# A two-block transformer forward pass on one core: last outputs in tiles of their own, first units side by side, the end reordered

## The chip, the cores and the metric

The kernel runs on 1 core of one Trainium2 chip. The metric is the device time of one execution in microseconds (us). The core's engines are TensorE (PE in the profile, with PEld for its weight loads), VectorE (DVE), ScalarE (ACT), GpSimd (POOL) and SyncE (SP), which issues the transfers of weights.

## The reference

One sequence of 512 tokens by 1024 features, all in float32. `first_block` runs a mixer (sparse attention and gated linear attention, merged), attention over a memory of 256 tokens, a gated FFN with a convolution over tokens, and a norm. `second_block` then runs retention, an FFN, stick-breaking attention, an FFN, and the final norm:

```python
def _rmsnorm(x, g):
    xf = x.astype(jnp.float32)
    y = xf * lax.rsqrt(jnp.mean(xf * xf, axis=-1, keepdims=True) + EPS)
    return (y * g.astype(jnp.float32)).astype(x.dtype)
...
    for i in range(DEPTH_2):
        j = i // N_MIXERS
        if i % N_MIXERS == 0:
            x = x + _retention(_rmsnorm(x, ret_norm[j]), ret_w_in[j], ret_w_out[j])
        else:
            x = x + _stick_breaking(_rmsnorm(x, sb_norm[j]), sb_w_in[j], sb_w_out[j])
        x = x + _conv_ffn(_rmsnorm(x, ffn_norm[i]), ffn_w_up[i], ffn_conv_w[i],
                          ffn_conv_b[i], ffn_w_down[i])
    return _rmsnorm(x, final_norm)
```

Retention has 4 heads with 256 key and 512 value features, stick-breaking attention 16 heads of 64 (here 8 pairs), each FFN 2816 hidden features (two up-projections, a convolution of width 3, a product, a down-projection).

## The kernel before, in words

**Number format.** Every float32 factor is split into a high part and a low part of a reduced type (fp32r). A product of two factors is then three matmuls: high by high (L184), high or low by low or high (L185, L186). In the rows, `xh` and `xl` are the parts of an activation, `wh` and `wl` those of a weight. In this text "a product" is one such matmul of 128x128 by 128x512.

**Activations.** x is kept transposed in SBUF: 8 tiles `x[0]` to `x[7]`, each 128 features by 512 tokens. For a norm, each is scaled by the norm's gain and split: ScalarE makes the high part (L276), VectorE the low part (L277). The parts of `x[0]` to `x[3]` lie in one tile (`xh_87`, `xl_89`), those of `x[4]` to `x[7]` in another (`xh_88`, `xl_90`). The scale of the norm (one number per token) comes later: ScalarE squares each x (L242), GpSimd adds the squares (L246, the last add on VectorE), TensorE adds over features ("column sums", L251), `rsqrt_cols` takes the root (L218 to L222, on VectorE with the power on GpSimd), TensorE broadcasts it over partitions (L231), ScalarE copies it to SBUF (`rB`, L269), and the products are scaled after the fact.

**Weights.** All weights are streamed once as "units" of 128x1024 (`wload`): SyncE starts the transfer into one of 2 raw buffers, ScalarE makes the high part (L157), VectorE the low part (L158), into rings of 3. A unit with 8 tiles of activations is 24 products into one PSUM bank (`fm_unit`). `norm_x` issues the splits, the first unit, the column sums, two more units, then the broadcast.

**Outputs.** Each stage ends with a projection whose results VectorE adds into x (L307). `out_proj2` takes half-length units, each for two outputs; `out_proj4` goes round four outputs in four banks.

**Stages.** `xat` (memory attention), `ffa` (first FFN), `ret` (retention), `ffb` (second FFN), `stk` (stick), `ffc` (third FFN). In retention each head makes keys, queries and values, the attention, and a gate; its result is transposed by TensorE and split into `yh`, `yl`; head 3 puts them into the tiles of `x[0]` to `x[3]`'s split. In stick the pairs 6 and 7 put their outputs into the tiles of `x[0]` and `x[1]`'s split.

**The end.** `down_halves` does the last down-projection's outputs 4 to 7 in two halves of 256 tokens, so that the final norm of half 0 (`finish`) runs beside the products of half 1. Five of eight outputs of a half are made by VectorE (L909), three by GpSimd (`POOL_TILES`, L907).

**What sets the order.** The kernel is written against a framework with a scheduler: a tool places each engine's instructions in an order of its own that respects the dependences between tiles and PSUM banks, and inserts the waits. So an engine's order differs from the order in the code, and a tile that is reused makes a wait. PSUM has 8 banks; the stages share them out by name (`pp` for products, `pa` for norms).

## Time and profile before

| | us |
|---|---|
| median of 3 runs | 2318.01 |
| lowest, highest of the runs | 2315.68, 2319.25 |
| the profiled execution | 2320.69 |
| its span in the trace | 2318.8 |
| TensorE busy | 2278.5 (98%) |
| VectorE busy | 1400.9 (60%) |
| ScalarE busy | 1022.5 (44%) |
| GpSimd busy | 194.5 (8%) |

The span is the time between the first and the last instruction in the trace. The mean granted clock of TensorE over the execution is 0.992 of full speed. A time line has one row per instruction or run of like instructions: start, duration, engine, line, operation, out <- in, and in brackets the idle time of the engine before it with what ended it. A TensorE row's duration overlaps its successor's, so the spacing of products is read from their starts.

### The profile page before, as it was taken

Reading aid. Unit: us, or ns where it says so; the run is one execution under the profiler, and the core shown is the slowest. Engines: PE = TensorE matmul, PEld = TensorE weight load, DVE = VectorE, ACT = ScalarE, POOL = GpSimd, SP = SyncE. Lnnn points to the kernel's source line nnn. Section 1 sums busy time; section 2 is a strip of 40 time slices with the busy share of each in tenths; the row PEclk is TensorE's granted clock in tenths of the full one; section 3 lists DMA queues with packets and bytes.
Section 4 is the critical chain, followed back from the end, with each engine's and each line's share of the span. In section 5 each row is a group of like instructions: output and inputs, shape, how many; then the busy total and the mean of one; then the engine's idle time right before and its main releaser. Section 6 shows DMA issues by size and latency. Waiting matters only on the chain.

```text
span 2318.8 us, 27885 instructions
## 1 busy us (share of the span) xinstructions
PE 2278.5 (98%) x10808; PEld 1880.6 (81%) x10808; DVE 1400.9 (60%) x2197; ACT 1022.5 (44%) x1665; POOL 194.5 (8%) x230
## 2 busy tenths in 40 slices
PE   9999999999999999999999999999999999999997
PEld 7787778877888888888887788888888887888886
DVE  5447875456545456445454674746577886747465
ACT  4345763444323244433333442424477884424243
POOL 2001110101000003000000100000121101000002
PEclk9989999999999999999999999999999999999998
DMA  5312133312232223222222233232343322232232
GB/s 160 91 55 63 37 119 96 123 63 95 97 100 94 98 88 114 90 91 78 81 96 73 82 100 99 92 100 93 98 126 93 92 67 80 100 100 92 100 93 71
DMA packets 66054, 213.41 MB, mean 92 GB/s; under 512 B 7793, under 2 KB 10114, under 8 KB 65794
## 3 DMA queue, kind: packets, MB, share of 16 engines
q1 hardware_dynamic: 60802, 203.24, 26.9%
q0 software_dynamic: 5120, 8.39, 1.6%
q8 instruction: 85, 1.39, 0.3%
q14 instruction: 47, 0.39, 0.1%
HBM read 201.11 MB, written 2.10 MB: 88 GB/s over the span
## 4 chain that ended last, share of the span: by engine, by line
PE 90%; DVE 4%; ACT 2%; POOL 1%; issue 1%; DMA 1%; SPq 0%; DVEq 0%; POOLq 0%; ACTq 0%
PE pp L184 26%; PE pp L186 26%; PE pp L185 26%; DVE wl L158 1%; PE po L701 1%; ACT pr L673 1%; DVE xl L277 1%; PE po L1163 1%; POOL pr L682 1%; PE pt L697 1%; PE pp L1070 1%; PE pp L1072 1%; PE pp L1071 1%; DVE x L307 1%; PE pa L1002 1%
## 5 line engine op out<-in xcount | busy, mean ns | idle before, releaser
L157 ACT ACTIVATE wh<-wr 128x1024 fp32r<-128x1024 f32 (+2 forms) x368 | 384.4, 1044 | 776.5 <-PE pp L185 609.0
L184 PE MATMUL pp<-xh,wh 128*128 128x512 f32 x1612 | 635.2, 394 | 3.4 <-ACT xh L276 3.2
L185 PE MATMUL pp<-xl,wh 128*128 128x512 f32 x1612 | 632.9, 393 | 3.6 <-DVE xl L277 3.6
L186 PE MATMUL pp<-xh,wl 128*128 128x512 f32 x1612 | 632.8, 393 | 0.0
L158 DVE TENSOR_TENSOR wl<-wr,wh 128x1024 fp32r<-128x1024 f32 (+2 forms) x368 | 451.6, 1227 | 211.5 <-ACT wh L157 185.2
L185 PEld LDWEIGHTS pp<-xl,wh 128*128 128x128 f32 x1612 | 305.0, 189 | 66.7 <-DVE xl L277 5.7
L184 PEld LDWEIGHTS pp<-xh,wh 128*128 128x128 f32 x1612 | 304.6, 189 | 66.7 <-ACT xh L276 4.4
L186 PEld LDWEIGHTS pp<-xh,wl 128*128 128x128 f32 x1612 | 304.6, 189 | 62.8 <-issue 0.9
L307 DVE TENSOR_TENSOR x<-x,pp 128x512 f32<-128x512 f32 x130 | 89.1, 686 | 230.2 <-PE pp L186 230.1
L184 PE MATMUL pp<-mid,wh 128*128 128x512 f32 x504 | 196.6, 390 | 0.3
L185 PE MATMUL pp<-mid,wh 128*128 128x512 f32 x504 | 196.1, 390 | 0.0
L186 PE MATMUL pp<-mid,wl 128*128 128x512 f32 x504 | 195.8, 389 | 0.0
L246 POOL TENSOR_TENSOR acc<-acc 128x512 f32<-128x512 f32 (+1 forms) x60 | 80.6, 1344 | 904.8 <-ACT acc L242 835.2
L185 PE MATMUL pp<-wl,xh 128*128 128x512 f32 (+1 forms) x320 | 123.0, 385 | 3.2 <-DVE wl L158 3.2
L184 PE MATMUL pp<-wh,xh 128*128 128x512 f32 (+1 forms) x320 | 121.8, 383 | 0.9 <-ACT wh L157 0.9
L186 PE MATMUL pp<-wh,xl 128*128 128x512 f32 (+1 forms) x320 | 122.1, 382 | 0.0
L184 PEld LDWEIGHTS pp<-mid,wh 128*128 128x128 f32 x504 | 94.6, 188 | 22.2 <-ACT mid L157 2.8
L185 PEld LDWEIGHTS pp<-mid,wh 128*128 128x128 f32 x504 | 94.6, 188 | 20.4 <-DVE mid L158 1.1
L186 PEld LDWEIGHTS pp<-mid,wl 128*128 128x128 f32 x504 | 94.6, 188 | 19.5
L157 ACT ACTIVATE mid<-wk 128x512 fp32r<-128x512 f32 x66 | 41.6, 631 | 124.4 <-DVE wk L874 108.7
L847 ACT ACTIVATE wk<-wk,vec 128x512 f32<-128x512 f32 x110 | 88.6, 809 | 6.6 <-DVE wk L861 5.2
L849 DVE SCALAR_TENSOR_TENSOR wk<-wk,vec 128x510 f32<-128x510 f32 x110 | 82.3, 750 | 3.6
(432 smaller groups left out, 3349.0 us busy)
## 6 DMA issues: line engine op xcount, KB each, us to landing
wr<-in_up SPq DMA_DIRECT2D x88, 512.0 KB, 3.3
wr<-in_w_up SPq DMA_DIRECT2D x44, 512.0 KB, 3.3
wr<-in_w_in_fm SPq DMA_DIRECT2D x32, 512.0 KB, 3.6
wr<-in_ret_vg SPq DMA_DIRECT2D x32, 512.0 KB, 3.3
wr<-in_down SPq DMA_DIRECT2D x32, 512.0 KB, 3.3
wr<-in_w_down SPq DMA_DIRECT2D x16, 512.0 KB, 3.3
wr<-in_ret_qk SPq DMA_DIRECT2D x16, 512.0 KB, 3.3
wr<-in_ret_out SPq DMA_DIRECT2D x16, 512.0 KB, 3.3
```

The costliest lines, as they stand in the source:

```text
L157: act.activation(hi, src, AF.Copy)
L158: dve.tensor_sub(lo, src, hi.bitcast(F32))
L184: pe.matmul(ps, sh, mh, start=first and i == 0, stop=False)
L185: pe.matmul(ps, sh, ml, start=False, stop=False)
L186: pe.matmul(ps, sl, mh, start=False, stop=last and i == n - 1)
L246: (dve if k == len(tiles) - 1 else pool).tensor_add(acc[:, :n], acc[:, :n], sq[:, :n])
L277: dve.scalar_tensor_tensor(lo, x, g, hi.bitcast(F32), op0=OP.mult, op1=OP.subtract)
L307: dve.tensor_add(xT[m], xT[m], ps)
L673: act.activation(dst, dst, AF.Exp, scale=-1.0, bias=nm[:, b:b + 1], accum_out=ss[:, g, b:b + 1])
L682: scaler(b).tensor_scalar(prs[g][b], prs[g][b], ss[:, g, b:b + 1], 1.0, op0=OP.mult, op1=OP.mult)
L847: act.activation(dst, src, AF.Identity, scale=V(wname, 2 * nw + j), bias=V(bname, j))
L849: dve.scalar_tensor_tensor(dst[:, 2:], src[:, :S - 2], V(wname, j), dst[:, 2:], op0=OP.mult, op1=OP.add)
```

## The change

It has four parts.

1. `norm_x` of the FFNs and of stick runs the first two units side by side (`two_units`): for each tile of activations, high part with both units' high and low parts, into two banks; then the 16 products with the low parts of the activations. The column sums come after both units. Memory attention keeps the old order.
2. Retention's values of a head lie in one tile for high and one for low parts; head 3's result goes into these and no longer into the tiles of `x[0]` to `x[3]`'s split. Stick's pairs 6 and 7 put their outputs into tiles of its values and queries.
3. Retention's head 0 makes the next head's keys ahead of its transposes; head 3 makes the first half of the previous head's output projection ahead of its own and the second half behind them.
4. The end: the norm scale of half 0 is computed during the products of half 1 but broadcast after the last of them; the last square is not added but summed by column sums of its own; VectorE's outputs take the broadcast from PSUM, six of eight outputs are VectorE's; 24 and 30 products of a 128x128 identity in bf16 (`warm`), whose results nobody reads, stand ahead of the column sums and of the broadcast of half 1.

```diff
-POOL_TILES = (2, 3, 5)
+POOL_TILES = (2, 5)
...
+    def two_units(srcs, h, tags):
+        us = [wload(u) for u in srcs]
+        pss = [bank(t) for t in tags[:2]]
+        for k in range(KD):
+            c = slice(k * P, (k + 1) * P)
+            for (hi, lo), ps in zip(us, pss):
+                pe.matmul(ps, hi[:, c], h[k][0], start=k == 0, stop=False)
+                pe.matmul(ps, lo[:, c], h[k][0], start=False, stop=False)
+        for k in range(KD):
+            c = slice(k * P, (k + 1) * P)
+            for (hi, lo), ps in zip(us, pss):
+                pe.matmul(ps, hi[:, c], h[k][1], start=False, stop=k == KD - 1)
+        return pss
+
-    def norm_x(gname, first, tags=("pp", "pp", "pp")):
+    def norm_x(gname, first, tags=("pp", "pp", "pp"), two=True):
...
-        ahead = []
+        ahead = two_units(first[:2], h, tags) if two else []
...
-        units(0, 1)
-        rcol, rB = norm_scale(xT, mid=lambda: units(1, 3))
+        units(len(ahead), 1)
+        rcol, rB = norm_scale(xT, mid=lambda: units(len(ahead), 3))
...
+        def warm(n):
+            ps = bank("pp")
+            for _ in range(n):
+                pe.matmul(ps[:, :P], identb, identb, start=True, stop=True)
...
+        def scales(ps, acc, last):
+            for x in range(n // P):
+                for i, t in enumerate((acc, last)):
+                    pe.matmul(ps[:, x:x + 1], t[:, x * P:(x + 1) * P], ones[:, 0:1], start=i == 0, stop=i == 1)
...
+        def outputs(half, rcol):
+            c = cols[half]
+            psb = bcast_cols(rcol[:, :n // P], n // P)
+            rB = sm.tile([P, S], F32, name="rB", bufs=1)
+            act.activation(rB[:, :n], psb[:, :n], AF.Copy)
...
-                        dve.scalar_tensor_tensor(y[:, j, :], xT[k][:, c], V("final_norm", k), rB[:, :n], op0=OP.mult,
+                        dve.scalar_tensor_tensor(y[:, j, :], xT[k][:, c], V("final_norm", k), psb[:, :n], op0=OP.mult,
                                                  op1=OP.mult)
...
-        finish(0, lambda: [product(1, i) for i in range(1, NHALF - 1)])
-        product(1, NHALF - 1)
-        finish(1)
+        r0 = scales(*sums(0))
+        for i in range(1, NHALF):
+            product(1, i)
+        s1 = sums(1)
+        outputs(0, r0)
+        warm(24)
+        r1 = scales(*s1)
+        warm(30)
+        outputs(1, r1)
...
+            vhl = [st.tile([P, NT, S], F32R, tag="v" + c, name="v" + c) for c in "hl"]
             for t in range(NT):
-                hi, lo = tiles(st, "v", 2, 8, F32R)
+                hi, lo = [x[:, t, :] for x in vhl]
...
-            if 0 < hd < 3:
-                out_proj2("ret_out", hd - 1, out_prev)
-            yh, yl = [st.tile([P, 4, S], F32R, tag="y" + c, name="y" + c) for c in "hl"] if hd < 3 else [x[0] for x in xhl]
+            if hd == 0:
+                ahead.append([fm_unit(wload(a["ret_qk"][10 + i]), h, KD) for i in range(2)])
+            else:
+                out_proj2("ret_out", hd - 1, out_prev, 0, 2 if hd == 3 else 4)
+            yh, yl = [st.tile([P, 4, S], F32R, tag=("y" if hd < 3 else "v") + c, name="y" + c) for c in "hl"]
...
-        out_proj2("ret_out", 2, ys[2])
+        out_proj2("ret_out", 2, ys[2], 2)
...
-            oh, ol = tiles(st, "os", 2, NOS, F32R) if pair < 6 else (xh[pair - 6], xl[pair - 6])
+            if pair < 6:
+                oh, ol = tiles(st, "os", 2, NOS, F32R)
+            elif pair == 6:
+                vt = st.tile([P, 3, 4, P], F32R, tag="vh", name="vh", bufs=2).rearrange("p t b d -> p t (b d)")
+                oh, ol = vt[:, 0, :], vt[:, 1, :]
+            else:
+                qt = st.tile([P, 2, S], F32R, tag="qh", name="qh", bufs=2)
+                oh, ol = qt[:, 0, :], qt[:, 1, :]
```

Three places show how the order moves. The first is VectorE from the last adds of retention's outputs into the second FFN (`x_3000` to `x_3014` in steps of 2 are x[0] to x[7]; `xl_89` and `xl_90` hold the low parts of x[0] to x[3] and x[4] to x[7]; `wl` is a weight unit's low part). Before:

```order
L307 TENSOR_TENSOR x_3006<-x_3006,pp 128x512
L158 TENSOR_TENSOR wl<-wr,wh 128x1024
L307 TENSOR_TENSOR x_3008<-x_3008,pp 128x512
L277 SCALAR_TENSOR_TENSOR xl_90<-x_3008,vec,xh_88 128x512
L307 TENSOR_TENSOR x_3010<-x_3010,pp 128x512
L158 TENSOR_TENSOR wl<-wr,wh 128x1024
L277 SCALAR_TENSOR_TENSOR xl_90<-x_3010,vec,xh_88 128x512
L307 TENSOR_TENSOR x_3012<-x_3012,pp 128x512
L277 SCALAR_TENSOR_TENSOR xl_89<-x_3000,vec,xh_87 128x512
L277 SCALAR_TENSOR_TENSOR xl_90<-x_3012,vec,xh_88 128x512
L277 SCALAR_TENSOR_TENSOR xl_89<-x_3002,vec,xh_87 128x512
L307 TENSOR_TENSOR x_3014<-x_3014,pp 128x512
```

With the change, the same place:

```order
L322 TENSOR_TENSOR x_3006<-x_3006,pp 128x512
L277 SCALAR_TENSOR_TENSOR xl_89<-x_3000,vec,xh_87 128x512
L277 SCALAR_TENSOR_TENSOR xl_89<-x_3002,vec,xh_87 128x512
L322 TENSOR_TENSOR x_3008<-x_3008,pp 128x512
L277 SCALAR_TENSOR_TENSOR xl_89<-x_3004,vec,xh_87 128x512
L277 SCALAR_TENSOR_TENSOR xl_89<-x_3006,vec,xh_87 128x512
L158 TENSOR_TENSOR wl<-wr,wh 128x1024
L322 TENSOR_TENSOR x_3010<-x_3010,pp 128x512
L277 SCALAR_TENSOR_TENSOR xl_90<-x_3008,vec,xh_88 128x512
L158 TENSOR_TENSOR wl<-wr,wh 128x1024
L322 TENSOR_TENSOR x_3012<-x_3012,pp 128x512
```

The low parts of x[0] to x[3] moved from behind the add of x[6] to ahead of the add of x[5].

The second is TensorE at the first FFN's first products (the numbers behind the names tell tiles and units apart; `xh0_87` and `xl0_89` are the tiles named above). Before, one unit:

```order
L184 MATMUL pp_4585<-xh0_87,wh_4580 128x512
L185 MATMUL pp_4585<-xl0_89,wh_4580 128x512
L186 MATMUL pp_4585<-xh0_87,wl_4581 128x512
L184 MATMUL pp_4585<-xh0_87,wh_4580 128x512
L185 MATMUL pp_4585<-xl0_89,wh_4580 128x512
```

With the change, the start of the block and the start of its second part:

```order
L286 MATMUL pp_4591<-xh0_87,wh_4580 128x512
L287 MATMUL pp_4591<-xh0_87,wl_4581 128x512
L286 MATMUL pp_4592<-xh0_87,wh_4586 128x512
L287 MATMUL pp_4592<-xh0_87,wl_4587 128x512
...
L291 MATMUL pp_4591<-xl0_89,wh_4580 128x512
L291 MATMUL pp_4592<-xl0_89,wh_4586 128x512
```

The products with low parts of the activations moved behind all products with high parts, and the second unit's weights (`wh_4586`, `wl_4587`) are read from the third product on.

The third is VectorE at the very end (`y` are outputs, `pa` the broadcast scale in PSUM, `rB` its copy). Before:

```order
L892 TENSOR_TENSOR x_3012<-x_3012,pp 128x256
L909 SCALAR_TENSOR_TENSOR y<-x_3000,vec,rB 128x256
L909 SCALAR_TENSOR_TENSOR y<-x_3002,vec,rB 128x256
L909 SCALAR_TENSOR_TENSOR y<-x_3008,vec,rB 128x256
L909 SCALAR_TENSOR_TENSOR y<-x_3012,vec,rB 128x256
L909 SCALAR_TENSOR_TENSOR y<-x_3014,vec,rB 128x256
L892 TENSOR_TENSOR x_3014<-x_3014,pp 128x256
L246 TENSOR_TENSOR acc<-acc 128x256
L218 TENSOR_SCALAR v<-pa 128x2
```

With the change:

```order
L246 TENSOR_TENSOR acc<-acc 128x256
L907 TENSOR_TENSOR x_3014<-x_3014,pp 128x256
L945 SCALAR_TENSOR_TENSOR y<-x_3000,vec,pa 128x256
L945 SCALAR_TENSOR_TENSOR y<-x_3002,vec,pa 128x256
L945 SCALAR_TENSOR_TENSOR y<-x_3006,vec,pa 128x256
L945 SCALAR_TENSOR_TENSOR y<-x_3008,vec,pa 128x256
L945 SCALAR_TENSOR_TENSOR y<-x_3012,vec,pa 128x256
L945 SCALAR_TENSOR_TENSOR y<-x_3014,vec,pa 128x256
L218 TENSOR_SCALAR v<-pa 128x2
```

The add of the last product moved ahead of half 0's outputs, and the last add of squares left its place between the last product's add and the norm scale.

## Rows read from the trace of the kernel before

**Rows 1.** Page: busy us (share of the span) and instructions of each engine

```profile
PE 2278.5 (98%) x10808; PEld 1880.6 (81%) x10808; DVE 1400.9 (60%) x2197; ACT 1022.5 (44%) x1665; POOL 194.5 (8%) x230
```

**Rows 2.** TensorE's waits: line waited for, releaser; us, times, longest us

```profile
PE pp L185 <- DVE xl L277: 3.6, 5, 1.2
PE pp L184 <- ACT xh L276: 3.2, 2, 2.8
PE pa L1036 <- DVE v L218: 1.7, 2, 0.9
PE pa L1036 <- DVE sg L1028: 1.3, 2, 0.6
```

**Rows 3.** Time line, TensorE, the end: start us, us, [idle before, releaser]

```profile
2305.84 0.99 PE L251 MATMUL pa<-cst,acc 128*128 128x1 f32 x4 [3.80 <-DVE acc L246]
2308.54 1.19 PE L231 MATMUL pa<-cst,rcol 128*128 128x128 f32 x4 [1.72 <-DVE rcol L222]
```

**Rows 4.** Stretches: us, busy by engine (instructions), granted clock, DMA share, GB/s

```profile
505.00:525.93 20.93, 20.93 (x89) 16.46 (x89) 14.10 (x16) 11.30 (x17) 6.40 (x4) 1.00 0.14 45
525.93:547.07 21.14, 19.71 (x83) 15.66 (x82) 10.42 (x14) 5.75 (x8) 5.12 (x4) 0.92 0.31 106
1296.71:1318.07 21.36, 18.83 (x83) 14.26 (x82) 11.29 (x17) 7.47 (x11) 2.37 (x2) 1.00 0.28 97
1662.71:1680.14 17.43, 17.43 (x83) 14.56 (x82) 6.20 (x10) 5.75 (x7) 1.05 (x2) 1.00 0.33 113
1932.63:1955.45 22.82, 19.82 (x83) 15.79 (x83) 9.55 (x15) 6.85 (x10) 2.32 (x2) 0.93 0.26 90
```

**Rows 5.** Time line, TensorE, first FFN

```profile
536.76 0.63 PE L186 MATMUL pp<-xh,wl 128*128 128x512 f32 x1
537.19 0.55 PE L184 MATMUL pp<-xh,wh 128*128 128x512 f32 x1
537.58 0.40 PE L185 MATMUL pp<-xl,wh 128*128 128x512 f32 x1
537.81 0.39 PE L186 MATMUL pp<-xh,wl 128*128 128x512 f32 x1
```

**Rows 6.** Time line, ScalarE, second FFN

```profile
1297.58 2.56 ACT L276 ACTIVATE xh<-x,vec 128x512 fp32r<-128x512 f32 x4 [1.98 <-DVE x L307]
```

**Rows 7.** Time line, TensorE, second FFN

```profile
1302.76 0.50 PE L185 MATMUL pp<-xl,wh 128*128 128x512 f32 x1 [0.72 <-DVE xl L277]
```

**Rows 8.** Time line, VectorE, ahead of the first FFN

```profile
525.14 2.32 DVE L158 TENSOR_TENSOR wl<-wr,wh 128x1024 fp32r<-128x1024 f32 x1
```

**Rows 9.** Time line, TensorE, third FFN

```profile
1935.58 0.73 PE L184 MATMUL pp<-xh,wh 128*128 128x512 f32 x2 [2.79 <-ACT xh L276]
```

**Rows 10.** Time line, VectorE, third FFN

```profile
1932.96 0.67 DVE L307 TENSOR_TENSOR x<-x,pp 128x512 f32<-128x512 f32 x1
```

**Rows 11.** Time line, VectorE, ahead of stick

```profile
1659.70 1.23 DVE L158 TENSOR_TENSOR wl<-wr,wh 128x1024 fp32r<-128x1024 f32 x1 [0.19 <-ACT wh L157]
```

**Rows 12.** Time line, TensorE, head 0 of retention

```profile
975.52 0.40 PE L184 MATMUL pp<-xh,wh 128*128 128x512 f32 x1
976.54 0.63 PE L1036 MATMUL pa<-cst,sg 128*128 128x128 f32 x4 [0.63 <-DVE sg L1028]
```

**Rows 13.** Time line, VectorE, the end

```profile
2300.36 3.96 DVE L909 SCALAR_TENSOR_TENSOR y<-x,vec,rB 128x256 f32<-128x256 f32 x5 [0.46 <-ACT rB L269]
2304.25 0.41 DVE L892 TENSOR_TENSOR x<-x,pp 128x256 f32<-128x256 f32 x1
2306.86 0.16 DVE L218 TENSOR_SCALAR v<-pa 128x2 f32<-128x2 f32 x1 [1.17 <-PE pa L251]
2310.27 3.56 DVE L909 SCALAR_TENSOR_TENSOR y<-x,vec,rB 128x256 f32<-128x256 f32 x5 [1.88 <-ACT rB L269]
```

**Rows 14.** Time line, TensorE, stick: a 128x128 bf16 product

```profile
1698.10 0.23 PE L1128 MATMUL zA<-maskb,identb 128*128 128x128 bf16 x1
1698.14 0.36 PE L1126 MATMUL zA<-qh,k 128*128 128x256 f32 x1
```

More of the change, by code (lines that the diff above doesn't have):

```diff
@@ L312, in out_proj, with out_proj2 @@
             add_x(m, ps)
-    def out_proj2(name, part, rhs, m0=0):
-        for m2 in range(m0, KD // 2):
+    def out_proj2(name, part, rhs, m0=0, m1=KD // 2):
+        for m2 in range(m0, m1):
             u = wload(a[name][part * 4 + m2])
@@ L793, in xattn @@
     def xattn(st, mkT, mv):
-        h, rcol, rB, ahead = norm_x("ln_x", [a["w_xq"][i] for i in range(3)])
+        h, rcol, rB, ahead = norm_x("ln_x", [a["w_xq"][i] for i in range(3)], two=False)
         os_ = []
@@ L892, in product, with sums @@
             dve.tensor_add(xT[m][:, c], xT[m][:, c], ps[:, :n])
[L894 to L901 removed]
+        def warm(n):
+            ps = bank("pp")
+            for _ in range(n):
+                pe.matmul(ps[:, :P], identb, identb, start=True, stop=True)
+        def sums(half):
+            c = cols[half]
+            ps = bank(cur["norm"])
+            acc = sumsq([x[:, c] for x in xT[:KD - 1]], n)
+            last = sm.tile([P, S], F32, tag="nrm", name="acc", bufs=3)
+            act.activation(last[:, :n], xT[KD - 1][:, c], AF.Square)
+            return ps, acc, last
+        def scales(ps, acc, last):
+            for x in range(n // P):
+                for i, t in enumerate((acc, last)):
+                    pe.matmul(ps[:, x:x + 1], t[:, x * P:(x + 1) * P], ones[:, 0:1], start=i == 0, stop=i == 1)
+            rcol = sm.tile([P, NT], F32, tag="rcol", name="rcol")
+            rsqrt_cols(rcol[:, :n // P], ps[:, :n // P], n // P, float(D), n // P)
+            return rcol
+        def outputs(half, rcol):
[3 more added lines that the diff above has]
+            act.activation(rB[:, :n], psb[:, :n], AF.Copy)
             for k2 in range(KD // 2):
```

13 lines of the change are left out of this document (4 added, 9 removed).

## The prediction

> **What bounds the kernel now.** I read the busy times first. TensorE is busy for 98% of the span [rows 1], so the other engines cost time only where TensorE waits for them or runs slowly because of them. The list of TensorE's waits, grouped by releaser, says where that is [rows 2]. It is short, and these kinds of wait in it belong to places that the change edits: low parts of the activations from the vector engine (3.6 us in five waits, one in the first FFN and four in the second), high parts from ScalarE (3.2 us in two, 2.8 of it in the third FFN), and the transposes of retention (1.7 and 1.3 us, half of each in head 0 and half in head 3). The time line of TensorE at the very end adds two more, 3.80 us before the last column sums and 1.72 before the last broadcast [rows 3].
>
> The waits do not tell all, so the table of stretches comes next [rows 4]. Its last four rows run from the first product of a stage to the broadcast of its norm scale, and hold the same work: three units of 24 products and the column sums. In the stick stage TensorE has no idle time there: 17.43 us of work in 17.43 us. That is the clean price. The three FFNs need 21.14, 21.36 and 22.82 us, so their excess is 3.71, 3.93 and 5.39 us. Each splits in two: idle time (21.14 - 19.71 = 1.43, 21.36 - 18.83 = 2.53, 22.82 - 19.82 = 3.00), and slow work (busy time above 17.43: 2.28, 1.40, 2.39). In the first and the third FFN the slow part has a visible cause: the granted clock of those stretches is 0.92 and 0.93, and product starts lie 0.43 us apart after the waits and 0.23 later [rows 5], the lower level of the clock (1.2 GHz) and then the full one (2.4 GHz). In the second the clock stays at 1.00, and the slow part is the restart after each of four waits.
>
> **The change part by part.** The base is the profiled execution, 2320.69 us with a span of 2318.8; it stands 2.68 us above the median of three runs, 2318.01.
>
> *The FFNs and stick.* Two things move. The last outputs of retention and of stick leave the tiles that hold the split of x0 to x3, so these splits need not wait until TensorE has read the old contents: in the second FFN ScalarE makes all four high parts in one burst only at 1297.58 [rows 6], after the first product's start at 1296.71, and the last wait for a low part ends at 1302.76 [rows 7], 6.05 us into the stage. And the first two units run side by side with the activations' low parts last: the 16 products that need these come after 32 others, 32 x 0.23 = 7.4 us into the stage. So the low parts are ready even if they come no earlier than now. What is late next is the second unit's weights, which are wanted 0.7 us into the stage instead of 24 x 0.23 = 5.5.
>
> First FFN: the vector engine's order there hardly changes, and it makes the second unit's low part from 525.14 for 2.32 us, to 527.46 [rows 8]. The block wants it at its fourth product, 525.93 + 3 x 0.23 = 526.6. So some 0.86 us of the 3.71 stays as a wait: **-2.85**. Ends: -1.2, if this wait still drops the clock and most of the 2.28 stays; -3.7, if nothing waits.
>
> Second FFN: the moved splits come ahead of two adds of outputs, and both weight parts stay ahead of the last splits. I keep 0.5 us of wait: **-3.4**, between -1.8 (half of the old waits come back with their restarts) and -3.9.
>
> Third FFN: TensorE starts only at 1935.58, after 2.79 us in which it waited for x0's high part [rows 9]. That part now comes early. But stick has only two of these banks, and the first unit's bank comes free with the add of x6, which now ends at 1932.96 + 0.67 = 1933.6 [rows 10]. After the change one split more stands ahead of it (an operation on 512 columns with two inputs, priced at 0.8 with the add's 0.67 as its lower bound), so it ends at about 1934.4, and the last product of stick ends near 1932.8. I keep 1.8 us, wait and restart: **-3.6**, between -1.5 (a clock drop remains beside the wait) and -5.4.
>
> Stick has no excess to give, and the weights that its block wants early are there: the second unit's low part is made from 1659.70 for 1.23 us [rows 11], 1.8 us before the first product at 1662.71. **0.**
>
> *Retention.* Head 0 waits 0.91 + 0.63 us and head 3 0.75 + 0.64 at the transposes, the 1.7 and 1.3 of the list; heads 1 and 2, where an output product already stands ahead of them, do not wait. A restart costs a little more: the start that follows the wait of 0.63 comes 1.02 us after the one before, not 0.23 [rows 12], so 0.79 is lost. Head 0 gets the next head's two key units as cover, 48 products or 11 us, and head 3 half an output product, 48 again: far more than the waits. In head 0 the later transposes may wait for low parts that the vector engine now makes behind the rotation of the new keys; I take off 0.3 there, and nothing for the value tiles joined into one per head. **-2.6**, between -1.2 (head 0 gives its gain back) and -3.6 (all four waits go with their restarts).
>
> *The end.* Now the vector engine does five outputs of half 0 in 3.96 us before it adds the last product into x7 at 2304.25, and the chain of the last norm stands behind that: column sums, the scale from 2306.86, outputs from 2310.27 for 3.56 us, to 2313.83 [rows 13]. After the change the add of x7 comes first, at about 2302.04 (2305.84 less the 3.80 of idling). Six outputs of half 0 follow, read from PSUM. Their price is not shown. Bounds: 0.41 us, the add of x7, which has one operand of the same shape in PSUM, and 3.56 / 5 = 0.71 for an output with both in SBUF beside GpSimd. I take 0.41, the nearer in operands. So the outputs end at 2302.45 + 6 x 0.41 = 2304.9; the column sums are there by then (a scale copy and a square of some 0.4 us each, then 0.99 at most). The scale's chain starts 1.95 us earlier than at 2306.86 and takes 1.68 to the broadcast at 2308.54, as before. From there to the outputs 1.73 us become about 1.0, since these no longer wait for the copy and the warm products are to keep the clock up. Six outputs take 2.46, to 2310.1: 3.7 us earlier. I take **-3.2**. With 0.71 per output in both halves and 1.35 behind the broadcast (1.73 without a copy of 0.38) it would be 2314.0, +0.2. The 54 warm products go in 0.04 us each in the one place where such a product is seen [rows 14], 2.2 us in two gaps that have room for them; at 0.1 us the second gap would overflow by some 2 us, so the upper end is +2.
>
> The Trainium skill (SBUF — State Buffer, Who interferes with whom) states that a vector instruction with at most one SBUF input does not contend with GpSimd, and one with two does while GpSimd reads. By it the outputs from PSUM cost what the add costs and this term would be -3.7; by the contended row it is +0.2.
>
> *Sum:* -2.85 - 3.4 - 3.6 - 2.6 - 3.2 = -15.65. 2320.69 - 15.65 = 2305.0 on the profiled level, and less 2.68 **2302.4** against the median of 2318.01. The products are the same in number, and no load of weights is added or taken away.
>
> **The rivals.**
>
> *The vector engine's queue keeps TensorE waiting (0.24).* The splits come early, but the wait for the second unit's weights and the one for a bank remain, and a wait of about 1 us is followed by the lower clock. For it: the first FFN dropped the clock with only 1.43 us idle. Against: the second idled 2.53 us at 1.00. Price: the slow parts of the first and third FFN come back, 2.28 + 2.39 = 4.7, and another 2 us of waits, so 9 is left of 15.65: **2309**, between 2306 and 2313.
>
> *The change does not reach its stages (0.08).* The early splits stand behind adds and weight parts in the vector engine's order, so that the waits only change their names and the FFNs give nothing; the end gives back what it gains, and retention alone keeps 2.6: **2315.4**. Against it, the order shows the splits moved ahead of adds.
>
> *Slower: side by side is slow in itself (0.04).* Four blocks of 48 products alternate between two banks. If alternating made TensorE start them at the lower clock's pitch, each would cost 0.43 - 0.23 = 0.20 us more, 192 x 0.20 = 38 us in all. It eats the gain from 15.65 / 38 on, a share of 0.41 of these products; at 0.6 of them the time is 2302.4 + 23 = **2325**. Against it, the output product ahead of the first FFN goes round four banks with no idle time at clock 1.00 (20.93 of 20.93 us, the first row of [rows 4]). The Trainium skill (TensorE: Matmul & The Clock Gate, A second HAM failure mode: psum-queue depth-cycling) describes a kernel that lost its clock again and again while it cycled through PSUM banks; the stretch just named speaks against that here.
>
> **How the numbers follow.** A measurement of this kernel can tell about 0.2%, 4.6 us, from no change: faster is under 2313.4, slower over 2322.6. The forecast has 0.64, with a range of its own of 2298 to 2307. The 80% range takes in most of the first rival and the far bounds of the sum's terms: 2297 to 2311. The forecast and nearly all of the first rival are faster (0.90); the second rival lies mostly within (0.07); most of the third is slower (0.03).
>
> **What would show it.** The stretches of the three FFNs, from the first product to the broadcast, fall to about 18.3, 18.0 and 19.3 us with a clock near 1.00; waits for low and high parts of the activations leave the list, and a wait for a weight's low part of about 0.9 us and one for an add of x appear. The transposes of heads 0 and 3 wait under 0.4 us in all. From the end of the last product to the span's end 16.8 us (2302.04 to 2318.8) become about 13.6. It is wrong if a stretch keeps a clock of 0.93, if the third FFN still starts over 2 us late, or if the last broadcast starts over 5.5 us after the last product.

## The result and the profile after

| | us |
|---|---|
| after, median of 6 runs | 2301.56 (2300.19 to 2302.92) |
| before, median of 6 runs | 2319.75 (2315.68 to 2320.77) |
| ratio, 95% interval | 0.9924 (0.9913 to 0.9936) |
| the profiled execution after, its span | 2300.85, 2299.0 |

The change makes the kernel faster by 0.76%, between 0.64 and 0.87%. The forecast was 2302.4, which is 15.65 us less than 2318.01, the median of the first three runs before; the two medians of six runs lie 18.19 us apart.

The table of stretches, cut as in [rows 4] from the first product of a stage to the broadcast of its norm scale, with the end in the fifth row:

```profile
522.78:541.08 18.30, 17.57 (x82) 14.33 (x81) 10.31 (x14) 5.46 (x7) 5.10 (x4) 1.00 0.27 89
1286.76:1305.08 18.32, 17.58 (x82) 14.33 (x81) 10.32 (x14) 5.46 (x7) 5.12 (x4) 1.00 0.27 87
1649.85:1667.12 17.27, 17.27 (x81) 14.41 (x80) 6.11 (x10) 5.57 (x6) 1.04 (x2) 1.00 0.22 77
1921.21:1938.61 17.40, 17.40 (x81) 14.49 (x81) 8.04 (x12) 5.34 (x7) 2.90 (x3) 1.00 0.27 89
2285.33:2299.00 13.67, 5.05 (x71) 4.70 (x69) 5.85 (x17) 1.07 (x3) 3.53 (x5) 0.77 0.44 153
```

The three FFNs take 18.30, 18.32 and 17.40 us instead of 21.14, 21.36 and 22.82, and the clock is 1.00 in all of them. The third has no idle time within the stretch; its wait now lies ahead of the first product. The 22.82 us of before, however, start 2.95 us ahead of the first product (1932.63 against 1935.58) and take the wait in. Cut in the same way, from 1920.07 where the next product would have started, the third takes 18.54 us after the change. The list of TensorE's waits tells what took the place of [rows 2]:

```profile
PE pp L287 <- DVE wl L158: 1.5, 2, 0.7
PE pp L286 <- DVE x L322: 1.0, 1, 1.0
PE pp L184 <- DVE x L322: 0.8, 1, 0.8
PE pa L231 <- DVE rcol L222: 0.8, 2, 0.6
```

No wait for a high or low part of the activations is left, and none at retention's transposes. There are two waits for the second unit's weights (L287, 0.73 and 0.74 us in the first and second FFN) and two for an add that holds a bank (L286, the third FFN's first product, and L184, stick's last output). On TensorE's time line in the first FFN's block the first row is such a wait, and the other three are from a stretch that alternates between two banks, two products at a time:

```profile
524.35 0.50 PE L287 MATMUL pp<-xh,wl 128*128 128x512 f32 x1 [0.73 <-DVE wl L158]
530.15 0.39 PE L286 MATMUL pp<-xh,wh 128*128 128x512 f32 x1
530.38 0.39 PE L287 MATMUL pp<-xh,wl 128*128 128x512 f32 x1
530.60 0.39 PE L286 MATMUL pp<-xh,wh 128*128 128x512 f32 x1
```

The starts lie 0.23 and 0.22 us apart, the pitch of the full clock. At the end, VectorE and then TensorE, beside [rows 13] and [rows 3]:

```profile
2285.42 0.42 DVE L907 TENSOR_TENSOR x<-x,pp 128x256 f32<-128x256 f32 x1 [0.69 <-PE pp L186]
2286.28 2.44 DVE L945 SCALAR_TENSOR_TENSOR y<-x,vec,pa 128x256 f32<-128x256 f32 x6 [0.44 <-ACT rB L935]
2288.63 0.15 DVE L218 TENSOR_SCALAR v<-pa 128x2 f32<-128x2 f32 x1
2291.52 2.44 DVE L945 SCALAR_TENSOR_TENSOR y<-x,vec,pa 128x256 f32<-128x256 f32 x6 [1.36 <-ACT rB L935]
```

```profile
2285.66 1.50 PE L912 MATMUL pp<-identb 128*128 128x128 bf16 x24
2287.00 1.00 PE L926 MATMUL pa<-cst,acc 128*128 128x1 f32 x8
2287.87 1.83 PE L912 MATMUL pp<-identb 128*128 128x128 bf16 x30
2290.30 0.68 PE L231 MATMUL pa<-cst,rcol 128*128 128x128 f32 x4 [0.60 <-DVE rcol L222]
```

Six outputs take 2.44 us (0.41 each) where five took 3.96 and 3.56, and the last broadcast's four products take 0.68 us where they took 1.19. But both runs of outputs still begin behind ScalarE's copy of the scale ("ACT rB").

The last output of VectorE is not what ends the program. GpSimd's outputs of half 1, and the instructions named DRAIN in its queue (how many; shortest, median and longest in ns; first and last start), first before and then after:

```profile
2310.32 2.45 POOL L907 TENSOR_TENSOR y<-gx,rB 128x256 f32<-128x256 f32 x3 [2.50 <-ACT rB L269]
L1366 POOLq DRAIN  x3: 34/93/7711, 2310.4 to 2318.6; - x3
```

```profile
2291.57 1.41 POOL L943 TENSOR_TENSOR y<-gx,rB 128x256 f32<-128x256 f32 x2 [1.99 <-ACT rB L935]
L1418 POOLq DRAIN  x3: 34/93/6671, 2291.6 to 2298.8; - x3
```

The longest drain, 7.71 us before and 6.67 us after, is the first of the three. It begins while these outputs are under way and ends 5.31 us after the last of them. In all fourteen profiles here it is 5.31 us, and the span ends 6.08 or 6.09 us after GpSimd's last output, while from VectorE's last output to the span's end it is anything from 4.21 to 6.05. SyncE's wait for the last transfer is over earlier in every profile (2296.8 after the change). So in every kernel here the span's end follows GpSimd's last output and not VectorE's. What sets the 5.31 us no run here shows.

For the experiments I measure by landmarks, since they are not touched by what happens elsewhere: the starts of the broadcasts (L231) on TensorE's time line, the start of the last product, and the end of VectorE's last output. The last column has the span's end. All in us, from one profile each. "Mixer" runs from the start to the broadcast after memory attention, and no kernel here changes anything in it.

| | mixer | to first FFN's | retention's second to second FFN's | stick's to third FFN's | last product to last output | memory attention's to last output | last product to span's end |
|---|---|---|---|---|---|---|---|
| before | 479.05 | 67.86 | 402.68 | 275.31 | 12.07 | 1834.79 | 17.08 |
| after | 475.90 | 65.18 | 395.68 | 271.49 | 8.86 | 1818.06 | 13.95 |
| e1_no_side | 475.95 | 67.80 | 396.69 | 271.38 | 8.86 | 1821.55 | 13.94 |
| e2_old_tiles | 475.20 | 65.20 | 396.13 | 274.97 | 8.86 | 1821.98 | 13.95 |
| e3_old_ret_order | 479.93 | 65.19 | 399.35 | 271.44 | 8.86 | 1821.63 | 13.95 |
| e4_old_end | 477.21 | 65.18 | 395.66 | 271.39 | 11.66 | 1820.73 | 16.66 |
| e5_no_warm | 480.27 | 65.23 | 395.70 | 271.51 | 9.37 | 1818.66 | 14.46 |
| e6_from_copy | 476.18 | 65.17 | 395.74 | 271.47 | 11.04 | 1820.24 | 15.25 |
| e7_blocks_of_four | 477.12 | 64.15 | 394.63 | 271.42 | 8.86 | 1815.96 | 13.96 |
| e8_other_banks | 477.60 | 65.20 | 395.78 | 270.12 | 8.86 | 1816.90 | 13.96 |
| e9_two_broadcasts | 475.31 | 65.21 | 395.79 | 271.38 | 8.23 | 1817.45 | 14.28 |
| e10_no_side_old_tiles | 476.08 | 67.83 | 398.62 | 273.79 | 8.86 | 1825.99 | 13.95 |
| e11_e10_again | 480.07 | 66.25 | 398.65 | 275.27 | 8.87 | 1825.87 | 13.97 |
| b2_all | 480.89 | 64.17 | 394.71 | 269.07 | 8.23 | 1813.00 | 14.27 |

The stretches that the change leaves alone agree within 0.1 us in all fourteen profiles: first FFN to retention's second broadcast 368.3, second FFN to stick 362.0, third FFN to the last product 346.5. From memory attention to the last output the change saves 16.73 us, to the span's end 16.64. The span fell by 19.79; the other 3.15 us lie in the mixer, which does not differ between the two kernels. The times of the experiments hold such differences of the mixer too, so what an edit is worth is read from the landmarks.

### The profile page after: what moved, and what is told of

Its sections match the earlier page's. It is cut to its first block, busy times and chain, and to the rows that moved or that the text cites. A ratio compares the mean times of both kernels' runs of the same rounds, so it can differ in the third digit from the quotient of the medians.

```text
span 2299.0 us, 28002 instructions
## 1 busy us (share of the span) xinstructions
PE 2271.2 (99%) x10870; PEld 1878.9 (82%) x10870; DVE 1395.4 (61%) x2199; ACT 1021.6 (44%) x1663; POOL 191.0 (8%) x226
## 4 chain that ended last, share of the span: by engine, by line
PE 93%; DVE 3%; ACT 2%; POOL 1%; issue 1%; DMA 0%; SPq 0%; DVEq 0%; POOLq 0%; ACTq 0%
PE pp L184 26%; PE pp L186 26%; PE pp L185 26%; DVE wl L158 1%; PE po L716 1%; ACT pr L688 1%; PE po L1208 1%; POOL pr L697 1%; PE pt L712 1%; DVE xl L277 1%; PE pp L1115 1%; PE pp L1116 1%; PE pp L1117 1%; PE pp L287 1%; PE pp L291 1%
## 5 line engine op out<-in xcount | busy, mean ns | idle before, releaser
L184 PE MATMUL pp<-xh,wh 128*128 128x512 f32 x1504 | 591.1, 393 | 0.0
L186 PE MATMUL pp<-xh,wl 128*128 128x512 f32 x1504 | 588.7, 391 | 0.0
L185 PE MATMUL pp<-xl,wh 128*128 128x512 f32 x1504 | 587.9, 391 | 0.0
L186 PEld LDWEIGHTS pp<-xh,wl 128*128 128x128 f32 x1504 | 283.1, 188 | 58.7 <-issue 0.9
L184 PEld LDWEIGHTS pp<-xh,wh 128*128 128x128 f32 x1504 | 283.0, 188 | 56.9 <-issue 0.8
L185 PEld LDWEIGHTS pp<-xl,wh 128*128 128x128 f32 x1504 | 283.1, 188 | 56.6
L184 PE MATMUL pp<-mid,wh 128*128 128x512 f32 x504 | 196.6, 390 | 0.3
L184 PE MATMUL pp<-wh,xh 128*128 128x512 f32 (+1 forms) x320 | 122.2, 384 | 0.8 <-ACT wh L157 0.8
L184 PEld LDWEIGHTS pp<-mid,wh 128*128 128x128 f32 x504 | 94.6, 188 | 22.3 <-ACT mid L157 2.8
```

The costliest lines, as they stand in the source:

```text
L184: pe.matmul(ps, sh, mh, start=first and i == 0, stop=False)
L185: pe.matmul(ps, sh, ml, start=False, stop=False)
L186: pe.matmul(ps, sl, mh, start=False, stop=last and i == n - 1)
```

## The experiments

**Undoing one part each.** The theory is that each part earns its gain in its own stage.

```diff
-    def norm_x(gname, first, tags=("pp", "pp", "pp"), two=True):
+    def norm_x(gname, first, tags=("pp", "pp", "pp"), two=False):
```

> The changed kernel, with the first two units of each FFN and of stick one after the other again, all else as changed. Theory A (each part earns its gain in its own stage, the new tiles and the order of the first units each do a share): the first FFN goes back to about 21 us from first product to broadcast, since its tiles were never shared; the second and third lose little, 18.5 to 19.5 us, because the splits of x0 to x3 stay early. Time 2301.6 + 2.8 + 1 + 1 = about 2306. Rival B (the order of the first units earns the whole gain of the FFNs): the second and third go back to 21.4 and over 21 us as well, time about 2311.

Measured: 2306.01, ratio to before 0.9947 (0.9932 to 0.9961). Its stretches of the first and second FFN:

```profile
522.82:543.75 20.93, 19.51 (x82) 15.40 (x81) 10.41 (x14) 5.58 (x8) 5.11 (x4) 0.92 0.31 103
1289.00:1308.79 19.79, 18.37 (x83) 14.63 (x82) 10.86 (x14) 5.58 (x8) 5.59 (x4) 1.00 0.36 121
```

The first FFN goes back to 20.93 us, as theory A has it. The second loses 1.01 us of landmarks, and the third nothing at all (271.38 against 271.49). The expected 18.5 to 19.5 us for the stretches of both is missed twice: the second takes 19.79, the third 17.36. So with the new tiles in place the order of the first units earns the first FFN's gain alone, a little of the second's, and none of the third's. The first FFN's clock is 0.92 in this profile, and the repeated program below shows what the lower clock costs there.

```diff
-            yh, yl = [st.tile([P, 4, S], F32R, tag=("y" if hd < 3 else "v") + c, name="y" + c) for c in "hl"]
+            yh, yl = [st.tile([P, 4, S], F32R, tag="y" + c, name="y" + c) for c in "hl"] if hd < 3 else [x[0] for x in xhl]
...
-            if pair < 6:
...
+            oh, ol = tiles(st, "os", 2, NOS, F32R) if pair < 6 else (xh[pair - 6], xl[pair - 6])
```

> The changed kernel, with the last outputs of retention and stick back in the tiles of x0 to x3's split, first units still side by side. Theory A: the first FFN stays at 18.3 us; the second and third start late or wait at once for the high parts of x0 to x3, 1 to 2.8 us each; time 2301.6 + 1.5 + 2.5 = about 2305.5. Rival B: since the low parts come last anyway, nothing is lost, time within 1 us of 2301.6.

Measured: 2304.10, ratio 0.9938 (0.9923 to 0.9953). The third FFN loses 3.48 us, the second only 0.45. The wait for high parts, and the third FFN's stretch from its first product:

```profile
PE pp L286 <- ACT xh L276: 4.2, 3, 2.8
1922.58:1941.88 19.30, 19.11 (x81) 15.36 (x82) 7.30 (x12) 4.65 (x6) 1.80 (x2) 0.91 0.15 51
```

The block waits for high parts from ScalarE (4.2 us, 2.8 of it ahead of the third FFN) and the clock of the third FFN's stretch is 0.91. Rival B falls in the third FFN. In the second it nearly holds, and the 1 to 2.8 us of theory A do not come there.

```diff
-            if hd == 0:
-                ahead.append([fm_unit(wload(a["ret_qk"][10 + i]), h, KD) for i in range(2)])
-            else:
-                out_proj2("ret_out", hd - 1, out_prev, 0, 2 if hd == 3 else 4)
+            if 0 < hd < 3:
+                out_proj2("ret_out", hd - 1, out_prev)
...
-        out_proj2("ret_out", 2, ys[2], 2)
+        out_proj2("ret_out", 2, ys[2])
```

> The changed kernel, with retention's units back in the old order around the transposes of heads 0 and 3. Theory A: the four waits at these transposes come back with their restarts, 3.6 us, and nothing else moves; time about 2305.2. Rival: what retention gained came from the tiles of the values and of head 3's output, and the time stays within 1 us of 2301.6.

Measured: 2307.39, ratio 0.9949 (0.9932 to 0.9965); 3.67 us more in retention and nothing anywhere else but in the mixer. The waits of before are back with the same totals, and the rival falls:

```profile
PE pa L1079 <- DVE v L218: 1.7, 2, 0.9
PE pa L1079 <- DVE sg L1071: 1.3, 2, 0.7
```

For the old end, the lines of `finish` replace `sums`, `scales`, `outputs` and `warm` (the reverse of the last part of the diff above).

> The changed kernel with the end of before. Theory A: the last output is again made 12.1 us after the start of the last product instead of 8.9, time about 2304.8. Rival (the end's part is given back in the stages ahead of it or in the last transfer): within 1 us of 2301.6.

Measured: 2306.84, ratio 0.9948 (0.9933 to 0.9962); 2.80 us more at the end, 11.66 instead of 8.86, and nothing elsewhere; to the span's end it is 2.71. The end of before took 12.07. The 0.41 between the two is in the last column sums, four products behind the same 3.80 us of idling, here from their start to the norm scale, first before, then in this kernel:

```profile
2305.84:2306.86 1.02, 0.99 (x4) 0.90 (x4) 0.00 (x0) 0.00 (x0) 0.00 (x0) 0.50 0.23 79
2290.36:2290.97 0.61, 0.58 (x4) 0.49 (x4) 0.00 (x0) 0.00 (x0) 0.00 (x0) 0.92 0.38 131
```

The granted clock was 0.50 in the one and 0.92 in the other.

**Do the order of the units and the tiles stand in for each other?** This kernel takes the edits of the first and second experiment together.

> Both parts undone together: first units one after the other and last outputs in the tiles of x0 to x3's split; retention's order and the end stay changed. Undone alone, they cost from retention's second broadcast to that of the second FFN 1.00 and 0.44 us. Theory A (each of the two is enough to hide most of the waits there, so they stand in for each other): together they cost 3.2 to 3.6 us there, four waits for low parts come back, and the time is about 2301.6 + 2.7 + 3.4 + 3.8 = 2311.5. Rival (the two shares add up): 1.4 us there, time about 2309.5.

Measured: 2309.67, ratio 0.9958 (0.9943 to 0.9973). From retention's second broadcast to the second FFN's it is 2.94 us over the changed kernel, a little under the expected 3.2 to 3.6. The two alone cost 1.01 and 0.45. The shares do not add up; either of the two edits hides most of these waits. The expected time was 1.8 too high. Most of that is the third FFN, which loses 2.30 us instead of the expected 3.8, for a reason that the next run shows.

> The kernel with both parts undone once more, for the clock alone. In its first profile the third FFN waited 2.79 us and kept a clock of 1.00, where the kernel before dropped to 0.93 after the same wait; the first FFN dropped to 0.92 after 0.37 and 1.05 us. If the wait's length decided, the third FFN would have to drop; if it is fixed for a program, this run shows 0.92, 1.00 and 1.00 again; if it is chance, one of the three differs from the first profile, and with it 1.5 us.

Measured: one run at 2312.81. The same program, the same waits, and another clock. TensorE's waits in the first FFN, and the one ahead of the third, first in the earlier profile, then in the later:

```profile
528.27 0.49 PE L184 MATMUL pp<-xh,wh 128*128 128x512 f32 x1 [0.37 <-ACT xh L276]
529.82 0.50 PE L185 MATMUL pp<-xl,wh 128*128 128x512 f32 x1 [1.05 <-DVE xl L277]
1928.57 0.73 PE L184 MATMUL pp<-xh,wh 128*128 128x512 f32 x2 [2.79 <-ACT xh L276]
```

```profile
532.26 0.51 PE L184 MATMUL pp<-xh,wh 128*128 128x512 f32 x1 [0.38 <-ACT xh L276]
533.80 0.50 PE L185 MATMUL pp<-xl,wh 128*128 128x512 f32 x1 [1.04 <-DVE xl L277]
1930.91 0.73 PE L184 MATMUL pp<-xh,wh 128*128 128x512 f32 x2 [2.75 <-ACT xh L276]
```

And the stretches of the first and third FFN to the broadcast, cut as in [rows 4], again the earlier profile first:

```profile
522.98:543.92 20.94, 19.52 (x82) 15.42 (x81) 10.40 (x14) 5.59 (x8) 5.10 (x4) 0.92 0.30 104
1925.62:1946.70 21.08, 18.07 (x81) 14.41 (x81) 9.55 (x15) 6.69 (x10) 2.32 (x2) 1.00 0.29 95
```

```profile
526.96:546.31 19.35, 17.93 (x81) 14.25 (x80) 10.41 (x14) 5.58 (x8) 5.12 (x4) 1.00 0.35 115
1928.00:1950.59 22.59, 19.63 (x81) 15.57 (x81) 9.51 (x15) 6.69 (x10) 2.32 (x2) 0.92 0.26 90
```

In the earlier one the clock was 0.92 in the first FFN and 1.00 in the third; in the later 1.00 and 0.92, each time after the same wait within 0.05 us. By the landmarks a fall costs 67.83 - 66.25 = 1.58 us in the first FFN and 275.27 - 273.79 = 1.48 in the third. So whether such a wait brings the lower clock differs between two executions of one program; its length alone does not decide.

**The end.** First without the 54 warm products, which are work that nothing reads.

```diff
-        warm(24)
         r1 = scales(*s1)
-        warm(30)
```

> The changed kernel without the 54 warm products of the end; their results are read by nobody. Theory A (they keep the clock up and cost nothing): the four products of the last broadcast start 0.21 us apart, as at the end of before, instead of 0.11, and the last output comes 0.3 to 0.5 us later; 9.3 us after the start of the last product instead of 8.9. Rival (they stand in front of the column sums and delay them): it comes up to 0.4 us earlier.

Measured: 2304.78, ratio 0.9935 (0.9921 to 0.9950); the last output comes 9.37 us after the last product's start, 0.51 later. TensorE:

```profile
2291.07 0.83 PE L926 MATMUL pa<-cst,acc 128*128 128x1 f32 x6 [0.66 <-ACT acc L920]
2294.77 1.19 PE L231 MATMUL pa<-cst,rcol 128*128 128x128 f32 x4 [2.87 <-DVE rcol L222]
```

The last broadcast takes 1.19 us again, as in [rows 3]; the granted clock during it is 0.50, where it is 1.00 in the changed kernel. The warm products earn half a microsecond, at the span's end too (14.46 against 13.95), and the column sums that wait behind them cost nothing, because VectorE comes to their result only after its outputs.

```diff
-                        dve.scalar_tensor_tensor(y[:, j, :], xT[k][:, c], V("final_norm", k), psb[:, :n], op0=OP.mult,
+                        dve.scalar_tensor_tensor(y[:, j, :], xT[k][:, c], V("final_norm", k), rB[:, :n], op0=OP.mult,
```

> The changed kernel with the vector engine's outputs taking the scale from its copy in SBUF instead of from PSUM; six of eight outputs remain the vector engine's. Theory A (two operands in SBUF make an output slow while GpSimd works): six outputs take 3.0 to 4.3 us instead of 2.44, in both halves, and the last output comes 1.2 to 3.6 us later. Rival (what made the outputs quick is the smaller share of GpSimd, or nothing but the count): 2.4 to 2.6 us, no later.

Measured: 2304.59, ratio 0.9934 (0.9920 to 0.9949); the last output comes 2.18 us later, 1.07 and 1.05 of it in the two runs of outputs. VectorE, and then the shortest, median and longest of the twelve outputs in ns, in this kernel and in the changed one:

```profile
2286.56 3.51 DVE L945 SCALAR_TENSOR_TENSOR y<-x,vec,rB 128x256 f32<-128x256 f32 x6 [0.44 <-ACT rB L935]
2292.93 3.49 DVE L945 SCALAR_TENSOR_TENSOR y<-x,vec,rB 128x256 f32<-128x256 f32 x6 [1.42 <-ACT rB L935]
L945 DVE SCALAR_TENSOR_TENSOR y<-x,vec,rB x12: 472/474/1054, 2286.6 to 2295.9; 128x256 f32<-128x256 f32 x12
```

```profile
L945 DVE SCALAR_TENSOR_TENSOR y<-x,vec,pa x12: 473/475/481, 2286.3 to 2293.5; 128x256 f32<-128x256 f32 x12
```

So reading the scale from the copy is not dearer in itself: most outputs take 0.47 us from either source, each overlapping the next. Slow are the first two of each run, 0.94 to 1.05 us, which run beside GpSimd's two outputs; the four behind them start 0.39 or 0.40 us apart. Theory A holds in its full wording: two operands in SBUF, while GpSimd works. GpSimd's two outputs take 1.60 and 1.58 us beside them, 1.42 and 1.41 in the changed kernel. The Trainium skill (SBUF — State Buffer, Who interferes with whom) puts such a slowing down to two SBUF inputs beside a GpSimd instruction that reads SBUF; these runs agree with it (up to 1.05 us from the copy and at most 0.48 from PSUM, both beside GpSimd). The span's end moves by 1.30 us only (15.25 against 13.95): GpSimd's outputs begin 1.12 us later and take 0.18 longer, and VectorE's slower second run is not on that path.

```diff
             psb = bcast_cols(rcol[:, :n // P], n // P)
+            psc = bank("pp")
+            for t in range(n // P):
+                pe.matmul(psc[:, t * P:(t + 1) * P], rcol[:, t:t + 1].to_broadcast([P, P]), ident, start=True, stop=True)
             rB = sm.tile([P, S], F32, name="rB", bufs=1)
-            act.activation(rB[:, :n], psb[:, :n], AF.Copy)
+            act.activation(rB[:, :n], psc[:, :n], AF.Copy)
```

> The changed kernel with the scale of the end broadcast twice, into one bank for ScalarE's copy and one for the vector engine's outputs. Theory A (the outputs still wait for the copy because both read one PSUM tile): the first output of each half starts when the broadcast is done, 0.4 us earlier in each half; last output 8.0 to 8.2 us after the start of the last product instead of 8.9. Rival (they wait for the broadcast itself): 8.9, or 9.1 with four more products in front.

Measured: 2302.06, ratio 0.9936 (0.9921 to 0.9952); VectorE's last output after 8.23 us instead of 8.86. VectorE, and GpSimd's last outputs:

```profile
2285.29 2.44 DVE L948 SCALAR_TENSOR_TENSOR y<-x,vec,pa 128x256 f32<-128x256 f32 x6
2287.92 0.16 DVE L218 TENSOR_SCALAR v<-pa 128x2 f32<-128x2 f32 x1 [0.19 <-PE pa L926]
2290.32 2.44 DVE L948 SCALAR_TENSOR_TENSOR y<-x,vec,pa 128x256 f32<-128x256 f32 x6 [0.87 <-PE pa L231]
2291.31 1.41 POOL L946 TENSOR_TENSOR y<-gx,rB 128x256 f32<-128x256 f32 x2 [2.44 <-ACT rB L938]
```

VectorE's wait for the copy is gone: the first run of outputs has no idle time ahead of it, and the second waits for the broadcast. It was an order in the program between two readers of one PSUM tile that made the outputs wait, and no engine that was late. Of the 0.7 to 0.9 us expected 0.63 arrives at VectorE's last output, because in half 0 the column sums are now late (0.19 of idling ahead of the scale). And the time gains nothing: GpSimd still takes the copy, the copy now stands behind four more products, and GpSimd's last output comes 8.19 us after the last product's start instead of 7.87. The span's end comes after 14.28 us instead of 13.95.

**What is left in the FFNs.**

```diff
-        for k in range(KD):
-            c = slice(k * P, (k + 1) * P)
-            for (hi, lo), ps in zip(us, pss):
+        for blocks in ([[(k, i)] for i in range(2) for k in range(KD // 2)], [[(k, 0), (k, 1)] for k in range(KD // 2, KD)]):
+            for k, i in sum(blocks, []):
+                c = slice(k * P, (k + 1) * P)
+                (hi, lo), ps = us[i], pss[i]
                 pe.matmul(ps, hi[:, c], h[k][0], start=k == 0, stop=False)
                 pe.matmul(ps, lo[:, c], h[k][0], start=False, stop=False)
```

> The changed kernel with another order in the block of two units: the first unit's 8 products with x0 to x3, then the second unit's 8, then the two side by side for x4 to x7, then the low parts. Theory A (what is left in the first two FFNs is the wait for the second unit's weights at the fourth product): the weights are wanted 1.1 us later, the two waits of 0.73 and 0.74 us go with their restarts, 0.9 us each, and the time is about 2299.8. Rival B (alternating between two banks itself costs something): the pitch of the products, 0.228 us, changes as well, in all four stages. Rival C: the waits come back at another product, time 2301.6.

Measured: 2299.67, ratio 0.9920 (0.9904 to 0.9937). The first and second FFN gain 1.03 and 1.05 us, stick and the third FFN, which have no such wait, nothing. The waits for weights are out of the list. Rival B falls: with half of the alternation gone, stick's 362.05 and the third FFN's 271.42 are those of the changed kernel.

```diff
-        out_proj4("sb_out", 1, [os_[p] for p in range(4, 8)], ["pp", "pp", "zA", "zA"])
+        out_proj4("sb_out", 1, [os_[p] for p in range(4, 8)], ["pp", "pp", "zA", "zA"], ["zB", "zB", "zA", "zA"])
```

(the second list is passed to `out_proj2`, which takes a bank of each name instead of `pp`)

> The changed kernel with stick's last four outputs in banks zB, zB, zA, zA instead of pp four times, so that neither its last output nor the first unit of the third FFN shares a bank with a fresh add. Theory A (what is left in the third FFN are two waits for an add that holds the bank, 0.80 and 0.99 us): both go with their restarts; TensorE is then about 2 us earlier at the block and waits up to 0.8 us for the second unit's weights; from stick's broadcast to the third FFN's 271.4 becomes 269.3 to 270.3. Rival (the vector engine's queue is the limit, not the bank): the waits change their names and 271.4 stays.

Measured: 2301.79, ratio 0.9929 (0.9916 to 0.9943). The waits for adds are gone, and the third FFN gains 1.37 us. In their place stands a third wait for the second unit's weights, 0.75 us:

```profile
PE pp L287 <- DVE wl L158: 2.2, 3, 0.7
```

The three edits together, with some of half 0's outputs behind half 1's norm scale:

> The changed kernel with three edits together: the block of two units begins with 8 products of one and 8 of the other unit, stick's last outputs go to other banks, and the end has two broadcasts and some outputs of half 0 behind the norm scale of half 1. Theory A: 1.0 us less in each of the first two FFNs, 2.1 in the third, 0.9 to 1.5 at the end: 5.0 to 5.6 less than the changed kernel, about 2296.3. Rival (a gain in one place is given back in the next): under 3 us less.

Measured by the landmarks: 5.06 us less than the changed kernel from memory attention to the last output (1813.00), of it 1.01, 0.97, 2.42 and 0.63 in the four places. The 2.42 in the third FFN is more than the other banks gave alone, since the third wait for weights goes too. Putting outputs behind the norm scale gave nothing beyond the two broadcasts. To the span's end it is 4.11 us less, since the end, as with the two broadcasts alone, ends later (14.27 against 13.95). But the time is 2300.51 in five runs (2297.24 to 2301.71), ratio 0.9920 (0.9908 to 0.9933), which these runs cannot tell from the changed kernel's. In its profile the mixer took 480.89 us, 5.0 more than in that of the changed kernel, and more than was won.

## Why the prediction was right, point by point

**The FFNs.** Forecast -2.85, -3.4 and -3.6, measured 67.86 - 65.18 = 2.68, 7.00 - 3.67 = 3.33 (the third experiment gives retention's share of the stretch), and 3.82. (Undoing both edits costs 2.94 in the second FFN; the 0.39 to 3.33 is not explained.) The wait for the second unit's weights was put at 0.86 and 0.5 us and is 0.73 and 0.74; the one for the bank was put at 1.8 with the restart, and is 0.99 us at the first product, with 0.80 one output earlier, where 0.33 stood before and the forecast saw no change. But one step of the reasoning was too firm. I took the slow clock of the first and the third FFN for a consequence of their waits. The repeated program shows that the same waits come with and without it. So about 1.5 us of the gain in each of the two was owed to the one profile of before from which I worked; by the repeated program, another execution could have given 1.1 instead of 2.68 in the first FFN (66.25 - 65.18). How often the clock falls there no run here shows.

**What carries which stage.** The forecast gave both edits a share in the second and third FFN. In the third, undoing the tiles loses 3.48 of the 3.82 us, about 1.5 of it the clock's, and undoing the order nothing; in the second each is enough for most of it.

**Retention.** Forecast -2.6, measured 3.67. This term was mis-sized: I took off 0.3 us for late low parts in head 0, which did not come (no wait at the transposes is in the list after), and counted the restarts only in the bound. From start to start [rows 12] each of the four waits cost about 0.9 us (3.67 / 4); the bound of 3.6 was the value.

**Stick.** Forecast 0, measured 0.02.

**The end.** Forecast -3.2, measured 12.07 - 8.86 = 3.21 to VectorE's last output and 17.08 - 13.95 = 3.13 to the span's end. That it fits so well is in part luck. The price of an output was right (0.41). The warm products go in 0.056 us each, not 0.04 (24 of them in the 1.34 us from 2285.66 to 2287.00), and still found room. The step "they no longer wait for the copy" was wrong, in both halves; the scale's chain began 1.57 us earlier against the last product, not 1.95, and from the broadcast to the outputs it took 1.22 us, not 1.0. On the other side, 0.41 of the gain is the low clock of the column sums in the one profile of before: against the old end put back, the change is worth 2.80, and 2.71 to the span's end. The choice of 3.2 between the bounds covered all this without naming it.

The path was wrong too. The working followed VectorE's outputs to the end and took GpSimd only as something that slows them. The span ends with GpSimd's drain. On that path, by the rows of GpSimd, its outputs of half 1 begin 6.47 us after the last product's start instead of 8.56, which is 2.09, and take 1.41 us instead of 2.45, which is 1.04, since there are two instead of three: 3.13 together. So the scale that comes earlier counts, and for it the cheap outputs of half 0, behind which the scale stands (where they took 1.07 us more, from the copy, GpSimd began 1.12 later). The cheap outputs of half 1 do not count, and the output taken from GpSimd is a third of the gain that the working had no term for. This split is worked out from the two profiles; no run changes the number of GpSimd's outputs alone.

**The sum.** Forecast 15.65, measured 16.73 by landmarks; 1.07 of the 1.08 between them is retention's. Up to 3.5 us of the 16.73 (some 1.5 each in the first and third FFN, 0.41 at the end) hang on the clock in the one profile of before.

**The rivals.** The first (waits go on and bring the lower clock) had the waits right, four of 0.7 to 1.0 us, but the clock of all four stretches is 1.00; by the repeated program that could have been otherwise in another execution. The second falls with the undone parts. The third falls with the pitch of 0.23 us in the alternating block and with the blocks of four. The rule of the Trainium skill that was weighed there (TensorE: Matmul & The Clock Gate, A second HAM failure mode: psum-queue depth-cycling) is not seen at work here: in all four stretches the clock is 1.00.

## What to carry to other kernels

When the operands of a first block arrive one by one, order its products by arrival and not by unit: what comes last is used last. A tile that takes a stage's last output and is the next stage's first input ties the two together; in the third FFN that cost 3.48 us, some 1.5 of it the clock's. Before speeding up the last work of a program, find the instruction that ends the span: here VectorE's last output came 0.63 us earlier in one kernel, and the span ended 0.33 us later. And when one edit is undone and little is lost, undo its neighbour too before calling it useless: two edits may each hide the same wait.

## What the runs showed of the hardware

The granted clock of TensorE is not fixed by the program. In the same program the wait pair 0.37 and 1.05 us was followed by the lower clock in one execution and by the full clock in the next, for 1.5 to 1.6 us of difference, and the wait of 2.79 us (2.75 in the second) likewise. At the end, the same column sums behind the same 3.80 us of idling ran at 0.50 in the profile of before and at 0.92 with the old end put back. The mixer, which is the same code in all fourteen profiles, took from 475.20 to 480.89 us. One stretch of it, in the kernel before, the changed one, and the twice profiled program:

```profile
120.00:150.00 30.00, 30.00 (x145) 24.76 (x144) 13.04 (x25) 12.17 (x18) 3.05 (x2) 0.81 0.13 36
```

```profile
120.00:150.00 30.00, 30.00 (x157) 24.69 (x158) 14.64 (x27) 12.99 (x19) 3.05 (x2) 0.91 0.13 37
```

```profile
120.00:150.00 30.00, 30.00 (x157) 24.75 (x157) 14.55 (x27) 13.00 (x19) 3.05 (x2) 0.91 0.12 36
```

```profile
120.00:150.00 30.00, 30.00 (x145) 24.88 (x146) 13.49 (x25) 12.68 (x19) 3.05 (x2) 0.83 0.11 36
```

TensorE is busy throughout, and the granted clock is 0.81, 0.91, 0.91 and 0.83. What brings it down there was not tried. For an edit worth under 5 us this scatter is larger than the edit in a handful of runs, and the landmarks, which agree within 0.1 us wherever neither the work nor the clock differs, are what tells.

The end of the program hangs on GpSimd: 5.31 us from its last output to the end of its drain and 6.08 or 6.09 to the span's end, in all fourteen profiles.
